# S5 coefficients of C in two buffers, the Toeplitz tile in a shared staging ring, and part of the mLSTM norm on ScalarE

## The chip, the cores and the metric

One core of one Trainium2 chip runs the whole kernel. The time is device microseconds (us) of one execution, inputs and outputs in the chip's memory; lower is better. The kernel before was timed three times. Each engine (TensorE or PE, VectorE or DVE, ScalarE or ACT, GpSimd or POOL, SyncE or SP) works through its own list of instructions in order; DMAs are issued from the lists of SP and ACT.

## What is computed

One step of a two-layer streaming encoder for 16 meta tokens, 2048 prompt frames and 8 sample streams of 16 frames. Layer 0 projects u = rmsnorm(x) into an S5 branch and an mLSTM branch with their gates; layer 1 has a retention and an RG-LRU branch. The parts that the change touches, cut to their core:

```python
# S5: complex diagonal state space, 32 groups of 16 channels, 64 states
_, _, h_re, h_im = lax.associative_scan(_cplx_combine, (a_re, a_im, bu_re, bu_im), axis=1)
y = einsum('btgp,gcp->btgc', h_re, c_re) - einsum('btgp,gcp->btgc', h_im, c_im)
y = gelu(y + d * u)
y = y * sigmoid(y @ w_glu + b_glu)
# mLSTM: 4 heads of 256, head norm over the head's 256 channels
mu = mean(h); var = mean(square(h - mu))
y = (h - mu) * rsqrt(var + EPS) * norm_w + skip * xc      # then times silu(zb)
```

## The kernel before, in words

The phases are the layer-0 projections of the S5 operands (`phase_in0`), the layer-0 projections of the mLSTM operands with the S5 branch woven in (`phase_l0`), the mLSTM chunks (`phase_mlstm`), the output projection (`phase_out0`) and layer 1 (`phase_in1`, `phase_ret`). Outside `phase_mlstm`, where PE's list is written out by hand, a scheduler of the framework sets the order of every engine's list from the program's dependencies and a model of durations, and the buffers of a tile name are handed out in the order in which the program asks for them.

**The projections of `phase_l0`.** The tokens are cut into six blocks (`ub`), two to a third. For each third and each of 8 column tiles `m` there are an xb part and a z part (`mtile`, L369 to L430): a weight slice is loaded by SP (L379), split by ACT and POOL into two fp32r halves, and for each block 8 × 3 matmuls of 384 columns (`mm3`, L121 to L125) fill a PSUM tile `pm`. The blocks of u come back from memory in `reload` (L461): three loads of 512 KB by SP (L467) into `ut1`, a ring of 4 buffers of 128×1024, then a cast on ACT (L105) and a subtraction on DVE (L109). `reload(2)` is called in the first third after m = 4, `reload(3)` at the beginning of the second third, after the first-block halves of two tiles.

**S5.** `s5` (L765) is a generator that is stepped once per tile from the third tile on (L506 to L510), so 14 steps belong to the first third: eight of the scan (loads, transposes L820, matmuls L827 into `ee`, scan on DVE L803 to L810), one that writes the states out (L836 to L863), and five of the eight y steps. The y part first loads C (L868, real and imaginary, each with transposes L871 and a copy L872) and d (L880, L881). For each q of 8, `toeplitz(q)` (L884) does:

- four small scalings into `cp` (L888 to L891), three DVE operations of 128×1088 into `ca` and a temporary (L895, L897, L899): the coefficients of C times powers;
- four matmuls (L904) into PSUM `pk`, a copy by ACT into `kp`, the d term on DVE (L908), and by SP one DMA of `kp` to memory (L909) and 8 DMAs back into the Toeplitz tile `tz` (L912), which shift each row.

The y loop (L916) then runs 20 matmuls per q (L925 to L931) on `tz`, `ca`, `ur` and `ee`, copies the result to `yst` and writes it out by ACT (L935). In the third third comes the GLU: loads of y (L950), the GLU weight into two buffers of the same ring `ut1` (`room`), Gelu, and projections with `mm3`.

**mLSTM.** Per chunk of 128 tokens, `ml_score_steps` builds scores, state weights and g = skip × xc on POOL (L1253). `ml_normed` (L1258) finds the head's mean and variance on DVE, rstd by a power on POOL (L1269), −mean × rstd on POOL (L1270), and y = scale × num + bias on ACT (L1271). `ml_gated_steps` adds and gates: DVE L1292 per k, then POOL multiplies by the gate for all 8 k at once (L1296).

Of the kernel before, what the change touches and what calls it, by code (L numbers as in the profile page):

```python
# [9 lines left out]
F32 = mybir.dt.float32  # L10
F32R = mybir.dt.float32r
I32 = mybir.dt.int32
AF = mybir.ActivationFunctionType
OP = mybir.AluOpType
# [9 lines left out]
KD = 8  # L24
# [329 lines left out]
def phase_l0(e):  # L354
# [103 lines left out]
    s5g = s5(e, ps)  # L458
    e.s5.loaded = False
    e.s5.room = lambda: xp.tile([128, 1024], F32R, name="ut1", bufs=4)  # L460
    def reload(bi):  # L461
        blk, b0, n = blks[bi]
        pool = e.ub_pool if bi % 3 < 2 else sb
        t = e.ub[bi] = pool.tile([128, 2, KD, 384], F32R, name=f"ub{bi % 3}", bufs=1)
        for c, nt, kind, row in blk:
            ur = xp.tile([128, KD, 128], F32, name="ut1", bufs=4)[:, :, :nt]
            nc.sync.dma_start(ur, e.u[:, :, c:c + nt])  # L467
            split(nc, t[:, 0, :, c - b0:c - b0 + nt], t[:, 1, :, c - b0:c - b0 + nt], ur)
# [296 lines left out]
def s5(e, ps):  # L765

    nc, v, tc = e.nc, e.nc.vector, e.tc
    p = e.s5
# [92 lines left out]
    with P(e, "s5y", side="right") as sb:  # L861

        pw, cc = p.pw, p.b  # L863
        for j, nm in enumerate(("re", "im")):
            cr = sb.tile([128, 4, 17, 16], F32, name="s5tm2").rearrange("p a b c -> p (a b c)")
            cr = cr[:, :512].rearrange("p (a b c) -> p a b c", a=4, b=2)
            for q in range(2):
                nc.sync.dma_start(cr[:, :, q, :], e.i["s5_c_" + nm].rearrange("a (m g) c p -> (g c) (a m) p", m=4))  # L868
            pc = ps.tile([128, 4, 128], F32, name="s5p", bufs=3)
            for m in range(4):  # L870
                nc.tensor.transpose(pc[:, m, :], cr[:, m].rearrange("p a b -> p (a b)"), e.ident)  # L871
            v.tensor_copy(cc[j].rearrange("p (m g) c -> p m (g c)", m=4), pc)  # L872


        d16 = sb.tile([128, 8], F32, name="s5d16")
        dd = sb.tile([128, 8, 16], F32, name="s5dd")
        v.memset(dd, 0.0)
        for j in range(4):
            js = slice(32 * j, 32 * j + 16)
            nc.sync.dma_start(d16[js], e.i["s5_d"].rearrange("a (q j c) -> j c (a q)", c=16, j=4)[j])  # L880
            v.tensor_tensor(dd[js], e.ident[js, None, js].to_broadcast([16, 8, 16]),  # L881
                            d16[js, :, None].to_broadcast([16, 8, 16]), op=OP.mult)

        def toeplitz(q):  # L884
            ur = s5_u(e, sb, q)
            gs = slice(4 * q, 4 * q + 4)
            cp = sb.tile([128, 2, 4, 17], F32, name="s5cp")
            v.tensor_copy(cp[UP, 0], pw[UP, 0, gs])  # L888
            v.tensor_scalar(cp[LO, 0], pw[LO, 1, gs], -1.0, None, op0=OP.mult)
            v.tensor_scalar(cp[UP, 1], pw[UP, 1, gs], -1.0, None, op0=OP.mult)  # L890
            v.tensor_scalar(cp[LO, 1], pw[LO, 0, gs], -1.0, None, op0=OP.mult)  # L891
            ca = sb.tile([128, 4, 17, 16], F32, name="s5ca")
            tmp = sb.tile([128, 4, 17, 16], F32, name="s5tm2")
            sh = [128, 4, 17, 16]
            v.tensor_tensor(ca, cp[:, 0, :, :, None].to_broadcast(sh), cc[0][:, gs, None, :].to_broadcast(sh),  # L895
                            op=OP.mult)
            v.tensor_tensor(tmp, cp[:, 1, :, :, None].to_broadcast(sh), cc[1][:, gs, None, :].to_broadcast(sh),  # L897
                            op=OP.mult)
            v.tensor_add(ca, ca, tmp)  # L899
            kp = sb.tile([128, 23, 16], F32, name="s5kp")  # L900
            v.memset(kp[:, 0:7, :], 0.0)
            pk = ps.tile([128, 256], F32, name="s5p", bufs=3)
            for j in range(4):
                nc.tensor.matmul(pk[32 * j:32 * j + 32], p.bb[:, 4 * q + j:4 * q + j + 2, :].rearrange("p a b -> p (a b)"),  # L904
                                 ca[:, j, 0:16, :].rearrange("p a b -> p (a b)"), start=True, stop=True,
                                 tile_position=(0, 32 * j), skip_group_check=True)
            nc.scalar.copy(kp[:, 7:23, :], pk.rearrange("p (a b) -> p a b", b=16))
            v.tensor_add(kp[:, 7, :], kp[:, 7, :], dd[:, q, :])  # L908
            nc.sync.dma_start(e.kp[q], kp)  # L909
            tz = sb.tile([128, 4, 16, 16], F32, name="s5tz")  # L910
            for k in range(8):
                nc.sync.dma_start(tz[16 * k:16 * (k + 1)],  # L912
                                  e.kp[q].rearrange("(g c) a b -> c g a b", g=4)[:16, :, 7 - k:23 - k, :])
            return ur, ca, tz

        for q in range(8):  # L916
            ur, ca, tz = toeplitz(q)
            for mh in range(2):
                yst = sb.tile([128, 4, NCH], F32, name="s5yst")
                for g0 in (0, 2):  # L920
                    py = ps.tile([128, 2, NCH], F32, name="s5p", bufs=3)
                    for j in range(2):
                        g = g0 + j
                        t0 = tz[:, g, 0:8, :].rearrange("p a b -> p (a b)")
                        t1 = tz[:, g, 8:16, :].rearrange("p a b -> p (a b)")  # L925
                        if mh == 0:
                            nc.tensor.matmul(py[:, j, :], t0, ur[:, 0, g, :], start=True, stop=False)
                        else:
                            nc.tensor.matmul(py[:, j, :], t1, ur[:, 0, g, :], start=True, stop=False)
                            nc.tensor.matmul(py[:, j, :], t0, ur[:, 1, g, :], start=False, stop=False)  # L930
                        nc.tensor.matmul(py[:, j, :],  # L931
                                         ca[:, g, 1 + 8 * mh:9 + 8 * mh, :].rearrange("p a b -> p (a b)"),
                                         ee[:, 4 * q + g, :], start=False, stop=True)
                    nc.scalar.copy(yst[:, g0:g0 + 2, :], py)
                nc.scalar.dma_start(e.ys[q // 2, mh, :, 4 * (q % 2):4 * (q % 2) + 4, :], yst)  # L935
            yield
    cls(e, "s5ee", "s5kb", "s5keep", "s5par")
    while not p.loaded:
# [200 lines left out]
def ml_score_steps(e, sb, lp, hp, pt, slots, res):  # L1139
# [67 lines left out]
    for i, slot in enumerate(slots):  # L1207
# [42 lines left out]
        p = c.p = sb.tile([128, H, 128], F32, name="m_p", bufs=nb(2))  # L1250
        v.tensor_tensor(p[:n, :, :n], pS[:n, :, :n], w[:n, :, :n], op=OP.mult)
        g = c.g = sb.tile([128, KD, 128], F32, name="m_kt" if dec else "m_g", bufs=nb(2))
        nc.gpsimd.tensor_tensor(g[:, :, :n], c.xc, e.pc[:, :, sk:sk + 1].to_broadcast([128, KD, n]), op=OP.mult)  # L1253
        res.append(c)
        yield

# [1 line left out]
def ml_normed(e, c, h, pn):  # L1258

    nc, v = e.nc, e.nc.vector  # L1260
    n, r0 = c.n, c.r0
    st = c.sb.tile([128, 6], F32, name="m_st", bufs=4)
    sm = c.sb.tile([128, 8], F32, name="m_sm", bufs=4)
    v.bn_stats(st[:n], pn[:n, 0:256])
    v.bn_aggr(sm[:n, 0:2], st[:n])
    v.tensor_scalar(sm[:n, 2:3], pn[:n, 256:257], -1.0, e.emcol[:n, r0 + h:r0 + h + 1], op0=OP.mult, op1=OP.max)
    v.tensor_scalar(sm[:n, 3:4], pn[:n, 256:257], sm[:n, 2:3], math.sqrt(EPS), op0=OP.max, op1=OP.mult)
    v.tensor_scalar(sm[:n, 4:5], sm[:n, 3:4], sm[:n, 3:4], sm[:n, 1:2], op0=OP.mult, op1=OP.add)
    nc.gpsimd.tensor_tensor(sm[:n, 5:6], sm[:n, 4:5], e.mhalf[:n, 0:1], op=OP.pow)  # L1269
    nc.gpsimd.tensor_scalar(sm[:n, 6:7], sm[:n, 0:1], sm[:n, 5:6], -1.0, op0=OP.mult, op1=OP.mult)  # L1270
    nc.scalar.activation(c.yn[:n, h, :], pn[:n, 0:256], AF.Identity, scale=sm[:n, 5:6], bias=sm[:n, 6:7])  # L1271


def ml_gated(e, c):
# [4 lines left out]
def ml_gated_steps(e, c):  # L1279

    nc, v = e.nc, e.nc.vector
    nw, g, n = e.row["ml_norm_w"], c.g, c.n
    zb = c.sb.tile([128, KD, 128], F32, name="m_rw" if c.dec else "m_zb", bufs=1 if c.dec else 2)
    nc.sync.dma_start(zb[:, :, :n], e.zb[:, :, c.c0:c.c0 + n])
    for q in range(2):
        py = c.pt("pa", 4, 128)
        for j in range(4):
            k = 4 * q + j
            nc.tensor.transpose(py[:, j, :n], c.yn[:n, k // 2, 128 * (k % 2):128 * (k % 2 + 1)], e.ident[:n, :n])
        for j in range(4):  # L1290
            k = 4 * q + j
            v.scalar_tensor_tensor(g[:, k, :n], py[:, j, :n], e.pc[:, k, nw:nw + 1], g[:, k, :n],  # L1292
                                   op0=OP.mult, op1=OP.add)
        if q == 0:
            yield
    nc.gpsimd.tensor_tensor(zb[:, :, :n], g[:, :, :n], zb[:, :, :n], op=OP.mult)  # L1296
    nc.scalar.dma_start(e.gb[:, :, c.c0:c.c0 + n], zb[:, :, :n])


# [872 lines left out]
```

## Time and profile before

| what | value |
|---|---|
| median of 3 runs | 3088.95 us (3086.74 to 3089.72) |
| the profiled execution: its time | 3077.24 us |
| its span, first to last instruction | 3075.5 us |
| mean granted TensorE clock, of 1 | 0.992 |
| PE busy | 2979.3 us, 97% of the span |
| DVE, ACT, POOL busy | 1671.9, 1059.5, 982.1 us |
| chain that ended last | PE 61%, DVE 6%, DMA 4%, ACT and POOL 1% each |

How to read it: the profile is one execution; it took 1.7 us more than its span and 11.7 us less than the median. PE is the engine with the least idle time, so a microsecond counts when PE stands still for it. The granted clock is a share of 2.4 GHz. In the tables of rows, "idle" is the time in which an engine stood still just before an instruction, with what released it.

### The profile page before, as it was taken

Reading aid. Unit: us, or ns where it says so; the run is one execution under the profiler, and the core shown is the slowest. Engines: PE = TensorE matmul, PEld = TensorE weight load, DVE = VectorE, ACT = ScalarE, POOL = GpSimd, SP = SyncE. Lnnn points to the kernel's source line nnn. Section 1 sums busy time; section 2 is a strip of 40 time slices with the busy share of each in tenths; the row PEclk is TensorE's granted clock in tenths of the full one; section 3 lists DMA queues with packets and bytes.
Section 4 is the critical chain, followed back from the end, with each engine's and each line's share of the span. In section 5 each row is a group of like instructions: output and inputs, shape, how many; then the busy total and the mean of one; then the engine's idle time right before and its main releaser. Section 6 shows DMA issues by size and latency. Waiting matters only on the chain.

```text
span 3075.5 us, 45329 instructions
## 1 busy us (share of the span) xinstructions
PE 2979.3 (97%) x17435; PEld 2696.1 (88%) x17435; DVE 1671.9 (54%) x3410; ACT 1059.5 (34%) x1860; POOL 982.1 (32%) x1160
## 2 busy tenths in 40 slices
PE   8999999998999989999999999999999999999999
PEld 7999989987988877777899999999998897888887
DVE  4845884454537772333446677767700036656563
ACT  4213443435254533211235555555511122121111
POOL 6305655445336751111111111111100024433431
PEclk9999999998999999999999999999999999999999
DMA  6447455556735557564441111111122167544442
GB/s 206 155 104 222 154 165 166 167 158 149 223 101 172 184 152 249 161 196 149 154 127 52 52 52 52 47 51 48 44 80 80 49 189 220 149 130 122 139 121 75
DMA packets 447298, 404.81 MB, mean 132 GB/s; under 512 B 43593, under 2 KB 392977, under 8 KB 447082
## 3 DMA queue, kind: packets, MB, share of 16 engines
q1 hardware_dynamic: 335340, 272.36, 31.2%
q10 hardware_dynamic: 111742, 129.56, 12.5%
q8 instruction: 137, 2.24, 0.3%
q14 instruction: 79, 0.65, 0.1%
HBM read 266.35 MB, written 135.49 MB: 131 GB/s over the span
## 4 chain that ended last, share of the span: by engine, by line
PE 61%; DVE 6%; DMA 4%; ACT 1%; issue 1%; POOL 1%; SPq 0%; DVEq 0%; POOLq 0%; ACTq 0%
PE p_pm L124 9%; PE p_pm L125 8%; PE p_pm L123 8%; PE r_pm L125 4%; PE r_pm L124 4%; PE r_pm L123 4%; PE pa L123 3%; PE pa L124 3%; PE pa L125 3%; PE pc L1388 1%; DVE p_d L1754 1%; PE pn L1385 1%; DVE p_xc L550 1%; PE r_o L1956 1%; DMA d_gb<-m_zb 1%
## 5 line engine op out<-in xcount | busy, mean ns | idle before, releaser
L123 PE MATMUL p_pm<-pu,p_wh 128*128 128x384 f32 (+1 forms) x1568 | 512.1, 327 | 0.2 <-ACT pu L105 0.2
L124 PE MATMUL p_pm<-pu,p_wh 128*128 128x384 f32 (+1 forms) x1568 | 511.8, 327 | 0.0
L125 PE MATMUL p_pm<-pu,p_wl 128*128 128x384 f32 (+1 forms) x1568 | 511.4, 326 | 0.0
L123 PE MATMUL pm<-ub,wh 128*128 128x384 f32 (+1 forms) x1136 | 377.2, 333 | 2.0 <-ACT vo L452 1.8
L124 PE MATMUL pm<-ub,wh 128*128 128x384 f32 (+1 forms) x1136 | 376.4, 331 | 1.6 <-DVE ub L109 1.6
L125 PE MATMUL pm<-ub,wl 128*128 128x384 f32 (+1 forms) x1136 | 372.9, 331 | 2.3 <-POOL wl L118 1.9
L123 PEld LDWEIGHTS p_pm<-pu,p_wh 128*128 128x128 f32 x1568 | 294.2, 188 | 1.8 <-issue 1.2
L124 PEld LDWEIGHTS p_pm<-pu,p_wh 128*128 128x128 f32 x1568 | 294.5, 188 | 1.0 <-issue 0.8
L125 PEld LDWEIGHTS p_pm<-pu,p_wl 128*128 128x128 f32 x1568 | 294.4, 188 | 0.0
L118 POOL TENSOR_TENSOR wl<-wr,wh 128x256 fp32r<-128x256 f32 x188 | 177.8, 976 | 203.7 <-ACT wh L105 203.7
L123 PEld LDWEIGHTS pm<-ub,wh 128*128 128x128 f32 x1136 | 214.4, 189 | 7.8 <-issue 4.0
L123 PE MATMUL r_pm<-roh,r_gh 128*128 128x512 f32 x544 | 218.8, 403 | 1.2 <-ACT roh L105 0.8
L125 PE MATMUL r_pm<-roh,r_gl 128*128 128x512 f32 x544 | 217.5, 401 | 1.5 <-DVE r_gl L109 1.5
L125 PEld LDWEIGHTS pm<-ub,wl 128*128 128x128 f32 x1136 | 214.4, 189 | 4.7 <-POOL wl L118 2.6
L124 PE MATMUL r_pm<-rol,r_gh 128*128 128x512 f32 x544 | 217.9, 401 | 0.4 <-DVE rol L109 0.4
L124 PEld LDWEIGHTS pm<-ub,wh 128*128 128x128 f32 x1136 | 214.7, 189 | 3.1 <-DVE ub L109 2.1
L109 POOL TENSOR_TENSOR p_wl<-p_wr,p_wh 128x1024 fp32r<-128x1024 f32 x34 | 81.8, 2406 | 385.2 <-ACT p_wh L105 385.2
L109 POOL TENSOR_TENSOR p_xcl<-p_xc,p_xch 128x384 fp32r<-128x384 f32 (+1 forms) x48 | 46.8, 976 | 245.5 <-ACT p_xch L105 209.0
L125 PEld LDWEIGHTS r_pm<-roh,r_gl 128*128 128x128 f32 x544 | 103.3, 190 | 24.0 <-DVE r_gl L109 2.4
L123 PEld LDWEIGHTS r_pm<-roh,r_gh 128*128 128x128 f32 x544 | 103.1, 190 | 22.7 <-ACT roh L105 1.3
L124 PEld LDWEIGHTS r_pm<-rol,r_gh 128*128 128x128 f32 x544 | 103.2, 190 | 21.0 <-DVE rol L109 0.7
L1754 DVE RECIPROCAL p_d<-p_d 128x384 f32<-128x384 f32 (+1 forms) x48 | 116.7, 2432 | 0.6
(731 smaller groups left out, 6751.0 us busy)
## 6 DMA issues: line engine op xcount, KB each, us to landing
wr<-in_ev_w_in_dram SPq DMA_DIRECT2D x47, 512.0 KB
p_wr<-in_od_w_in_dram SPq DMA_DIRECT2D x40, 512.0 KB
d_in<-p_o ACTq DMA_DIRECT2D x80, 192.0 KB
m_rw<-d_grow SPq DMA_DIRECT2D x18, 512.0 KB
s5u<-d_ua SPq DMA_DIRECT2D x32, 274.0 KB
d_v<-vo ACTq DMA_DIRECT2D x68, 128.0 KB
m_va<-d_v SPq DMA_DIRECT2D x17, 512.0 KB
d_h<-o_x ACTq DMA_DIRECT2D x17, 512.0 KB
```

The costliest lines, as they stand in the source:

```text
L109: (nc.gpsimd if pool else nc.vector).tensor_tensor(l, x, h, op=OP.subtract)
L118: nc.gpsimd.tensor_tensor(out[:, c], a[:, c], b[:, c], op=op)
L123: nc.tensor.matmul(out, a[0], b[0], start=start, stop=False, **kw)
L124: nc.tensor.matmul(out, a[0], b[1], start=False, stop=False, **kw)
L125: nc.tensor.matmul(out, a[1], b[0], start=False, stop=stop, **kw)
L550: v.tensor_scalar(out, x(3), pc[:, m, cw + 3:cw + 4], pc[:, m, cb:cb + 1], op0=OP.mult, op1=OP.add)
L1385: nc.tensor.matmul(pn[:n], c.qs[:, 2 * h + k, :n], ct[h][:, k, :], start=False, stop=k == 1)
L1388: nc.tensor.matmul(pc, c.kw[:n, h, 128 * k:128 * (k + 1)], c.va[:n, h, :], start=True, stop=True)
L1754: v.reciprocal(d[:, :n], d[:, :n])
L1956: nc.tensor.matmul(po, qk[:, h, :], S[:, h, :], start=False, stop=True)
```

## The change

Five edits in the S5 and mLSTM code:

1. `ca` gets two buffers instead of one.
2. `tz` no longer has a buffer of its own (`s5tz`, one buffer) but is taken from `e.s5.stage`, which hands out a buffer of the `ut1` ring, the ring of the reloads.
3. `yst` holds two groups instead of four, in two buffers; y is written out by 4 DMAs per q instead of 2 (32 instead of 16).
4. In the mLSTM, POOL's g product and POOL's gate product are each done in two halves; the first half of the gate product is issued before the step's yield.
5. −mean × rstd moves from POOL to ACT as two operations: −mean (needs only the mean), then times rstd.

```diff
@@ phase_l0
     e.s5.room = lambda: xp.tile([128, 1024], F32R, name="ut1", bufs=4)
+    e.s5.stage = lambda: xp.tile([128, 1024], F32, name="ut1", bufs=4)
@@ s5, toeplitz(q)
-            ca = sb.tile([128, 4, 17, 16], F32, name="s5ca")
+            ca = sb.tile([128, 4, 17, 16], F32, name="s5ca", bufs=2)
...
-            tz = sb.tile([128, 4, 16, 16], F32, name="s5tz")
+            tz = p.stage().rearrange("p (g a b) -> p g a b", g=4, a=16)
@@ s5, y loop
             for mh in range(2):
-                yst = sb.tile([128, 4, NCH], F32, name="s5yst")
                 for g0 in (0, 2):
+                    yst = sb.tile([128, 2, NCH], F32, name="s5yst", bufs=2)
...
-                    nc.scalar.copy(yst[:, g0:g0 + 2, :], py)
-                nc.scalar.dma_start(e.ys[q // 2, mh, :, 4 * (q % 2):4 * (q % 2) + 4, :], yst)
+                    nc.scalar.copy(yst, py)
+                    gs = slice(4 * (q % 2) + g0, 4 * (q % 2) + g0 + 2)
+                    nc.scalar.dma_start(e.ys[q // 2, mh, :, gs, :], yst)
@@ ml_score_steps
-        nc.gpsimd.tensor_tensor(g[:, :, :n], c.xc, e.pc[:, :, sk:sk + 1].to_broadcast([128, KD, n]), op=OP.mult)
+        for q in range(2):
+            qs = slice(4 * q, 4 * q + 4)
+            nc.gpsimd.tensor_tensor(g[:, qs, :n], c.xc[:, qs], e.pc[:, qs, sk:sk + 1].to_broadcast([128, 4, n]),
+                                    op=OP.mult)
@@ ml_normed
+    nc.scalar.mul(sm[:n, 6:7], sm[:n, 0:1], -1.0)
     nc.gpsimd.tensor_tensor(sm[:n, 5:6], sm[:n, 4:5], e.mhalf[:n, 0:1], op=OP.pow)
-    nc.gpsimd.tensor_scalar(sm[:n, 6:7], sm[:n, 0:1], sm[:n, 5:6], -1.0, op0=OP.mult, op1=OP.mult)
-    nc.scalar.activation(c.yn[:n, h, :], pn[:n, 0:256], AF.Identity, scale=sm[:n, 5:6], bias=sm[:n, 6:7])
+    nc.scalar.activation(sm[:n, 7:8], sm[:n, 6:7], AF.Copy, scale=sm[:n, 5:6])
+    nc.scalar.activation(c.yn[:n, h, :], pn[:n, 0:256], AF.Identity, scale=sm[:n, 5:6], bias=sm[:n, 7:8])
@@ ml_gated_steps, per q
+        qs = slice(4 * q, 4 * q + 4)
+        nc.gpsimd.tensor_tensor(zb[:, qs, :n], g[:, qs, :n], zb[:, qs, :n], op=OP.mult)
         if q == 0:
             yield
-    nc.gpsimd.tensor_tensor(zb[:, :, :n], g[:, :, :n], zb[:, :, :n], op=OP.mult)
```

The ring's buffers go round in the order of the calls, so five `tz` now stand between the three loads of `reload(2)` and those of `reload(3)`. The lists show what the scheduler makes of it; line numbers of the S5 part are higher by one in the changed kernel. **SP's list** around the second third's reload; `ut_3875`, `ut_3879`, `ut_3883` are `reload(2)`, `ut_4945`, `ut_4949`, `ut_4953` are `reload(3)` before:

```order
L467 DMA ut_3875<-d_u 128x8x128
L467 DMA ut_3879<-d_u 128x8x128
L467 DMA ut_3883<-d_u 128x8x128
L467 DMA ut_4945<-d_u 128x8x128
L761 DMA s5u<-d_ua 128x548 x2
L779 DMA s5rt<-d_rot 128x2x516
L379 DMA wr_2863<-in_ev_w_in_dram 128x8x128
L379 DMA wr_3056<-in_ev_w_in_dram 128x8x128
L467 DMA ut_4949<-d_u 128x8x128
L441 DMA wv_3500<-in_ml_wv_dram 128x2x256
L467 DMA ut_4953<-d_u 128x8x128
```

After the change `reload(3)` is `ut_4965`, `ut_4969`, `ut_4973`, and `ut_4628` and `ut_4837` are the `tz` of q = 3 and q = 4:

```order
L913 DMA ut_4628<-d_kp 16x4x256 x8
L762 DMA s5u<-d_ua 128x548 x2
L910 DMA d_kp<-s5kp 128x368
L913 DMA ut_4837<-d_kp 16x4x256 x8
L468 DMA ut_4965<-d_u 128x8x128
L468 DMA ut_4969<-d_u 128x8x128
L468 DMA ut_4973<-d_u 128x8x128
L762 DMA s5u<-d_ua 128x548 x2
```

The loads of block 3 moved from right behind those of block 2, in the midst of the S5 scan, to behind the round trips of q = 0 to 4. **PE's list** where the y of a q ends and where `pk` of another stands, before:

```order
L929 MATMUL s5p<-s5u,s5tz 128x137
L930 MATMUL s5p<-s5u,s5tz 128x137
L931 MATMUL s5p<-s5ee,s5ca 128x137
L124 MATMUL pm_5675<-ub_3874,wh_5667 128x384
...
L125 MATMUL pm_5701<-ub_4944,wl_5668 128x384
L427 MATMUL pg_4871<-xc_5656,gw 8x192
L904 MATMUL s5p<-s5ca,s5bb 32x256 x4
L427 MATMUL pg_4871<-xc_5656,gw 8x192 x3
```

After the change, from the last projection on block 2 (`ub_3874`) to the first on block 3 (`ub_4964`); the left-out rows hold the y of q = 0 and of q = 1 to 4, with the `pk` of q = 2 to 4 between them, and nothing else:

```order
L125 MATMUL pm_4938<-ub_3874,wl_4931 128x384
L828 MATMUL s5p<-s5u,s5bat 128x137 x8
L846 MATMUL s5p<-ident,s5bat 128x128 x2
L856 MATMUL s5p<-ident,s5fin 32x128
L872 MATMUL s5p<-ident,s5tm_4151 128x128 x4
L872 MATMUL s5p<-ident,s5tm_4160 128x128 x4
L905 MATMUL s5p<-s5ca,s5bb 32x256 x4
L928 MATMUL s5p<-s5u,ut_4203 128x137
...
L905 MATMUL s5p<-s5ca,s5bb 32x256 x4
L928 MATMUL s5p<-s5u,ut_4348 128x137
...
L905 MATMUL s5p<-s5ca,s5bb 32x256 x4
L123 MATMUL pm_4977<-ub_4964,wh_4894 128x384
```

The pieces of S5 that lay between projections moved into one run of rows with no projection between them. **DVE's list** after the change, around the coefficients of the next q (`s5cp`, `s5ca`) and the d term (`s5dd`) of the q before it:

```order
L902 MEMSET s5kp 128x112
L896 TENSOR_TENSOR s5ca<-s5cp,s5b_1471 128x1088
L900 TENSOR_TENSOR s5ca<-s5ca,s5tm_4614 128x1088
L889 COPY s5cp<-s5pw 64x68
L890 TENSOR_SCALAR s5cp<-s5pw 64x68
L891 TENSOR_SCALAR s5cp<-s5pw 64x68
L909 TENSOR_TENSOR s5kp<-s5kp,s5dd 128x16
L892 TENSOR_SCALAR s5cp<-s5pw 64x68
```

Two products and three scalings for a later q now stand ahead of the d term, L909, that releases the round trip.

## Rows read from the trace of the kernel before

**Rows 1.** The page, part 1: busy us (share of the span) and instructions.

```profile
PE 2979.3 (97%) x17435; PEld 2696.1 (88%) x17435; DVE 1671.9 (54%) x3410; ACT 1059.5 (34%) x1860; POOL 982.1 (32%) x1160
```

**Rows 2.** Waits of PE, whole span: line waited for, us in total, times, longest.

```profile
PE pm L123 <- ACT xb L397: 11.8, 3, 5.6
...
PE pn L1383 <- ACT m_yn L1271: 8.7, 3, 4.8
...
PE s5p L845 <- DVE s5bat L842: 4.0, 1, 4.0
...
PE pa L1248 <- DVE m_g L1292: 2.6, 4, 0.9
```

**Rows 3.** Timeline of PE, 425 to 434 us: start, duration, instruction, [idle before].

```profile
425.40 0.33 PE L123 MATMUL pm<-ub,wh 128*128 128x384 f32 x1
...
431.69 2.03 PE L827 MATMUL s5p<-s5u,s5bat 128*128 128x137 f32 x16
```

**Rows 4.** Timeline of DVE, 415 to 502 us.

```profile
415.36 1.22 DVE L109 TENSOR_TENSOR ub<-ut,ub 128x1024 fp32r<-128x1024 f32 x1
...
436.32 1.02 DVE L803 TENSOR_TENSOR s5tm<-s5ee,s5rt 64x516 f32<-64x516 f32 x1
...
451.34 1.03 DVE L842 TENSOR_TENSOR s5bat<-s5tm,s5ed 128x256 f32<-128x256 f32 x1
...
474.73 1.29 DVE L897 TENSOR_TENSOR s5tm<-s5cp,s5b 128x1088 f32<-128x1088 f32 x1
...
477.57 1.28 DVE L899 TENSOR_TENSOR s5ca<-s5ca,s5tm 128x1088 f32<-128x1088 f32 x1
```

**Rows 5.** Timeline of SP's queue, 465 to 644 us.

```profile
465.58 0.97 SPq L868 DMA_DIRECT2D s5tm<-in_s_c_im_dram  x2
...
487.91 5.08 SPq L912 DMA_DIRECT2D s5tz<-d_kp  x8
...
508.69 0.32 SPq L909 DMA_DIRECT2D d_kp<-s5kp  x1
...
511.71 5.49 SPq L912 DMA_DIRECT2D s5tz<-d_kp  x8
...
638.36 0.32 SPq L909 DMA_DIRECT2D d_kp<-s5kp  x1
640.21 3.60 SPq L912 DMA_DIRECT2D s5tz<-d_kp  x8
```

**Rows 6.** Waits of SP's queue, 400 to 700 us.

```profile
SPq L868 <- PE s5p L871: 4.0, 1, 4.0
```

**Rows 7.** Timeline of PE, 495 to 499 us: the y of q = 0.

```profile
495.17 0.47 PE L927 MATMUL s5p<-s5u,s5tz 128*128 128x137 f32 x2 [1.21 <-DMA s5tz<-d_kp]
...
498.42 0.42 PE L123 MATMUL pm<-ub,wh 128*128 128x384 f32 x1
```

**Rows 8.** PE by line, 425 to 600 us: busy us, mean ns | idle before.

```profile
L904 PE MATMUL s5p<-s5ca,s5bb 128*32 128x256 f32 x40 | 3.7, 389 | 0.0
```

**Rows 9.** Stretches: window, us, busy us PE, PEld, DVE, ACT, POOL, PEclk, DMA share, GB/s.

```profile
693.00:770.00 77.00, 62.67 (x425) 58.03 (x424) 33.98 (x55) 45.65 (x82) 44.60 (x80) 0.89 0.67 146
705.00:727.00 22.00, 9.13 (x46) 7.46 (x47) 5.71 (x13) 13.80 (x21) 8.70 (x16) 0.61 1.07 196
825.00:840.00 15.00, 15.00 (x89) 14.94 (x88) 12.73 (x37) 2.43 (x4) 5.38 (x7) 1.00 1.10 336
```

**Rows 10.** Timeline of PE behind the longest idle time of that stretch.

```profile
722.32 0.59 PE L123 MATMUL pm<-wvh,xbh 128*128 128x264 f32 x1 [5.03 <-ACT xb L397]
722.70 0.42 PE L124 MATMUL pm<-wvl,xbh 128*128 128x264 f32 x1
...
726.46 0.28 PE L123 MATMUL pm<-wvh,xbh 128*128 128x264 f32 x1
```

**Rows 11.** POOL by line, 850 to 1165 us, the mLSTM chunks: busy us, mean ns | idle before.

```profile
L1253 POOL TENSOR_TENSOR m_g<-m_xc,pc 128x1024 f32<-128x1024 f32 (+1 forms) x17 | 31.7, 1866 | 13.7 <-PE pm L125 13.7
L1270 POOL TENSOR_SCALAR m_sm<-m_sm 128x1 f32<-128x1 f32 (+1 forms) x68 | 19.6, 290 | 4.2
```

## The prediction

> **What bounds the kernel now.** Page first: PE is busy 97% of the span [rows 1], so what PE waits for is the next view. Its waits are short and few [rows 2]: of those that the change touches there are 4.0 us for the S5 state-out (L845), 8.7 us for the normed value of the mLSTM (L1383 behind ACT's L1271) and 2.6 us for the gated one (L1248). No line of the change stands in a long wait, so there is little to win. What can be lost is larger: PE's list is fixed, and in `phase_l0` the S5 branch is cheap only because projections lie between its pieces. The timelines of PE, DVE and SP from 425 us on show that: after `kp` is sent off, `tz` is there only some 9 us later [rows 5], and PE spends those with projections. Look in the rows at the times between one engine's last piece and the next engine's first.
>
> **Part 1, the reload behind the round trips.** The ring has four buffers, handed out in the program's order: three to `reload(2)`, then five to `tz` of q = 0 to 4, then three to `reload(3)`. Its loads so stand in SP's list behind the fifth round trip, and the first projection on block 3 stands in PE's list behind y(q = 4). Between the last projection on block 2 and that one, PE's list has only S5, each piece waiting for the one before. All times are from the span's start.
>
> - *Where it begins.* Before, PE goes to the third tile of the second third at 425.4 [rows 3]. After, it stands there before the last scan. Its matmuls (L827) take 2.03 [rows 3]; they begin after ACT's copies, at about 429 (estimate: the place of q = 7 in the lists), and the two copies of `ee` follow by 431.5. The last scan and the state-out on DVE last from 436.32 to 452.37, 16.05, of which 1.5 was a convolution [rows 4]: 14.5, so T = 446 (443 to 448).
> - *T to y(q = 0).* The load of imaginary C was issued at 465.58, 13.2 behind the end of L842 (452.37), of which 4.0 was a wait for PE [rows 5, 6]: T + 9.2. Landing 2.2 (the last of the first `tz` DMAs was issued by 492.99 and y began at 495.17 [rows 5, 7]), transposes and copy 1.3, the products L897 and L899 1.29 and 1.28 [rows 4]: T + 15.3. In DVE's list the scalings and two products of q = 1 stand ahead of the d term L908 of q = 0: 3.4 plus 0.2, and 0.6 for what ACT and PE put between: T + 19.5. Then the round trip D: from `kp`'s issue to the first of 8 `tz` issues 1.85 to 3.02, the issues 3.60 to 5.49, landing 2.2 [rows 5]. Of the eight pairs three lie near 1.9 and five at 2.6 to 3.0, and where SP has nothing else the issues take 3.6, so I take 2.7 + 3.6 + 2.2: D = 8.5 (7.65 to 10.7). y(q = 0) begins at T + 28 = 474 (26 to 33 behind T).
> - *Each further link.* Between 495.17 and 498.42, 14 of y's 20 matmuls run, 0.232 each, so the whole takes 4.64 at full clock [rows 7]. After an idle time the clock was low: in 705 to 727 the granted clock is 0.61, and after 5.03 of idle the same matmul shows 0.42 instead of 0.28 until 726.3, four us later [rows 9, 10]. A y that begins after a wait I put at 6.6: 4 us at half speed, then 2.64 (4.64 to 9.3). Behind it on DVE, since `ca` has two buffers and the new coefficients need that of q − 2: two products of 1.29 [rows 4] ahead of the d term, then 0.8 for `pk`'s rest, the copy and L908, then D. 6.6 + 2.6 + 0.8 + 8.5 = 18.5 (15.7 to 23.4). Four of them: 74, so y(q = 4) begins at 548.
> - *The reload.* Its three loads go out right behind the last `tz`, 2.2 ahead of y(q = 4). 1.57 MB take 4.7 us at the 336 GB/s of one stretch and 10.8 at the 146 of another [rows 9]; the queue is otherwise empty, so I take 7, nearer the first. Cast 1.05 (estimate, near the subtraction's) and subtraction 1.22 [rows 4]. PE goes on at 548 − 2.2 + 7 + 2.3 = 555.1 (553 to 559).
> - *What of it isn't lost.* PE did S5 work there that it needn't do later: L827 2.03, six `pk` at 0.74 (3.7 for five in that stretch [rows 8]) 4.4, five y at 4.64 23.2, small transposes some 2: 31.6.
>
> Net: 555.1 − 425.4 − 31.6 = **+98.1**.
>
> On the longest piece the Trainium skill, "DMA: Bandwidth & Descriptors", section "Anatomy of one DMA — SWDGE (gpsimd) path", gives one DMA about 2.0 us fixed, mostly the receipt, plus bytes over 436 GB/s. The landing of 2.2 agrees with it; by it D would be 2.0 + 3.6 + 2.0 = 7.6, five links 4.5 less, and the median below some 4.5 lower.
>
> **Part 2, what goes away.** The wait for the state-out, 4.0 [rows 2], and the 1.21 before the first y [rows 7] lie inside the new stall: −5.2.
>
> **Part 3, later S5.** The y of q = 5 to 7 still go by the ring, but with projections between them: +3 (0 to 8), the 8 being one D. `yst` in two halves costs 16 more issues on ACT; ACT is busy 34% and those lie beside PE: 0. If that cover goes, each is some 0.4 (the issue time of SP's DMAs, 3.60 / 8 [rows 5]), so 16 × 0.4 = 6 on ACT, in the stall's slack. Cold clock at the restart: 4 us at half speed, +2 (0 to 4) [rows 10].
>
> **Part 4, mLSTM.** POOL loses 68 instructions of 0.29 us [rows 11] in a chain power, product, ACT; ACT gets two small ones, of which one waits for nothing that PE needs. The halves of L1253 (1.87 each time [rows 11]) let the power in between them, and the first half of the gate product overlaps DVE's second. All of this can win at most what PE waits there, 8.7 + 2.6 = 11.3 [rows 2]; I take half, −6 (0 to −11.3). Could it lose? The extra ACT operation with the scale waits for the power and stands ahead of the next evictions: 68 of an estimated 0.2 to 0.3, in a chain that loses 0.29 in exchange; nothing net.
>
> **The sum.** 98.1 − 5.2 + 3 + 2 − 6 = +92 on 3077.24: 3169. The profiled execution lies 11.7 below the median; the same difference on the median gives 3088.95 + 92 = **3181**.
>
> **The rivals.**
>
> 1. *Shorter links (3144).* D at its lower end and less, as SP has nothing else in its list there: 8 issues at 0.3 each 2.4, both landings 1.85: 6.1, and each y at 4.64; so a link is 2.4 + 2.0 = 4.4 less; four links and the first D: −20. And the GLU, whose loads come earlier, no longer leaves PE idle in 693 to 770, where 77.00 − 62.67 = 14.3 are [rows 9]. 92 − 20 − 14 − 3 = 55. For: the stretch is empty of other transfers. Against: `kp`'s landing took 2.7 in most of the eight, some in quiet stretches.
> 2. *Longer links (3212).* The clock stays low for all five y and the small transposes (9.3 instead of 6.6 or less, five times, +13), D at 10 (+7), the GLU's loads now stop PE too (32 issues at 0.35, up to +11). 92 + 31 = 123: 3212. For: 0.61 of clock in a stretch with idle times of 5 us [rows 9]. Against: y is 4 us long, and there is other work at either end.
> 3. *Faster (3058).* The S5 branch is ready earlier, so the GLU is under the projections and PE loses none of the 14.3 [rows 9], nor 5.2 of S5 waits, nor 11.3 in the mLSTM: −31. It decides only if the chain up to the block-3 loads ends before PE runs out of its own work: T to restart must cost no more than 31 of real work plus 31 saved, by about 488. T is 446, so five links would need to fit in 42 us with the first already 28: 3.5 us a link, below the bare landing and y. Near impossible by rows 5.
> 4. *No change (3083).* The moved loads don't stop PE, as if blocks 2 and 3 were still loaded together. Only the −6 is left. PE's list speaks against it: nothing but S5 stands there.
>
> **How the numbers follow.** The forecast, with its own range 3156 to 3200, gets 0.68; shorter links 0.15; longer 0.12; faster 0.03; no change 0.02. The predicted time is 3181. The range goes to the nearer rivals: 3145 to 3219 leaves out little of the shorter and the far end of the longer, with the cases of no change and faster. A measurement of this kernel can tell about 0.2%, 6 us, from no change. Faster by more: 0.03. Within: 0.02. Slower by more: 0.95.
>
> **What would show it.** Right: a gap in PE's rows from about 425 to 555 with only L828, L846, L872, L905 and L928 to L932 in it, granted clock well below 1, in which PE waits for `tz` from `kp` five times, some 8 to 12 us each; the loads of block 3 at about 545; PE's idle time up by some 90 to 100 us and nearly all of it there. In the mLSTM the waits of PE for L1271 under 8.7. Wrong: projections between the y pieces; the first load on block 3 near its old place; links under 13 us or over 22; an idle time of this size elsewhere, above all in the GLU or the mLSTM.

## The result, and the profile after

The changed kernel takes 3155.97 us (median of 4 runs, 3151.03 to 3160.21) against 3088.12 for the kernel before: a ratio of 1.0222 (95% interval 1.0207 to 1.0236), **67.9 us slower**. 3181 was forecast, with 3145 to 3219 as the range. The profiled execution took 3154.68 us, its span 3153.0, which is 77.5 longer than the span of before; this one lies only 1.3 below its median, where that of before lay 11.7 below the 3088.95 of the first three runs.

Page, part 1, of the changed kernel, and below it PE's waits over the whole span:

```profile
PE 2992.8 (95%) x17435; PEld 2706.2 (86%) x17435; DVE 1657.1 (53%) x3410; ACT 1090.5 (35%) x2006; POOL 959.2 (30%) x1124
```

```profile
PE s5p L928 <- DMA ut<-d_kp: 50.3, 5, 10.3
PE s5p L846 <- DVE s5bat L843: 10.1, 1, 10.1
...
PE s5p L872 <- DMA s5tm<-in_s_c_im_dram: 6.9, 1, 6.9
...
PE s5p L905 <- DVE s5ca L900: 3.4, 1, 3.4
...
PE pn L1390 <- ACT m_yn L1277: 3.7, 2, 2.7
```

PE does the same 17435 instructions. It is busy 13.5 us longer than in [rows 1] and idle 64.0 longer (3153.0 − 2992.8 = 160.2 against 3075.5 − 2979.3 = 96.2): together the 77.5. Five waits for the Toeplitz tile make 50.3, where [rows 7] show one of 1.21; with the state-out, the load of C and the coefficients the four S5 lines make 70.7. The wait for the mLSTM's normed value fell from 8.7 [rows 2] to 3.7.

The timeline of PE in the stretch (start, duration, instruction, idle before):

```profile
422.19 1.09 PE L828 MATMUL s5p<-s5u,s5bat 128*128 128x137 f32 x8
...
435.50 0.69 PE L846 MATMUL s5p<-ident,s5bat 128*128 128x128 f32 x2 [10.13 <-DVE s5bat L843]
...
444.33 1.09 PE L872 MATMUL s5p<-ident,s5tm 128*128 128x128 f32 x4 [6.85 <-DMA s5tm<-in_s_c_im_dram]
448.85 1.08 PE L905 MATMUL s5p<-s5ca,s5bb 128*32 128x256 f32 x8 [3.43 <-DVE s5ca L900]
459.40 0.80 PE L928 MATMUL s5p<-s5u,ut 128*128 128x137 f32 x2 [9.47 <-DMA ut<-d_kp]
...
466.15 0.64 PE L905 MATMUL s5p<-s5ca,s5bb 128*32 128x256 f32 x8
476.84 0.80 PE L928 MATMUL s5p<-s5u,ut 128*128 128x137 f32 x2 [10.06 <-DMA ut<-d_kp]
...
494.24 0.80 PE L928 MATMUL s5p<-s5u,ut 128*128 128x137 f32 x2 [10.20 <-DMA ut<-d_kp]
...
511.47 0.80 PE L928 MATMUL s5p<-s5u,ut 128*128 128x137 f32 x2 [10.19 <-DMA ut<-d_kp]
...
528.78 0.80 PE L928 MATMUL s5p<-s5u,ut 128*128 128x137 f32 x2 [10.34 <-DMA ut<-d_kp]
...
535.86 0.62 PE L123 MATMUL pm<-ub,wh 128*128 128x384 f32 x2 [0.24 <-ACT ub L105]
```

Five y begin 17.44, 17.40, 17.23 and 17.31 apart, and the first projection on block 3 (L123) comes 7.1 after the fifth. In the window from the first to the last of these rows the granted clock is 0.67 and PE is busy 42.2 of 114:

```profile
422.00:536.00 114.00, 42.20 (x279) 36.77 (x278) 45.76 (x90) 14.26 (x34) 1.64 (x3) 0.67 0.37 101
```

SP's queue shows what PE waits for:

```profile
452.17 0.34 SPq L910 DMA_DIRECT2D d_kp<-s5kp  x1
454.04 3.61 SPq L913 DMA_DIRECT2D ut<-d_kp  x8
...
469.49 0.32 SPq L910 DMA_DIRECT2D d_kp<-s5kp  x1
471.38 3.60 SPq L913 DMA_DIRECT2D ut<-d_kp  x8
...
526.67 2.61 SPq L468 DMA_DIRECT2D ut<-d_u  x3
```

From the issue of `kp` (452.17, 469.49) to y (459.40, 476.84) are 7.23 and 7.35 us. The loads of block 3 go out at 526.67, right behind the fifth tile's.

### The profile page after: what moved, and what is told of

It reads as the page before. It is cut to its first block, busy times and chain, and to the rows that moved or that the text cites. A ratio compares the mean times of both kernels' runs of the same rounds, so it can differ in the third digit from the quotient of the medians.

```text
span 3153.0 us, 45528 instructions
## 1 busy us (share of the span) xinstructions
PE 2992.8 (95%) x17435; PEld 2706.2 (86%) x17435; DVE 1657.1 (53%) x3410; ACT 1090.5 (35%) x2006; POOL 959.2 (30%) x1124
## 4 chain that ended last, share of the span: by engine, by line
PE 73%; DVE 13%; DMA 7%; issue 2%; ACT 2%; POOL 1%; SPq 1%; ACTq 1%; DVEq 0%; POOLq 0%
PE p_pm L124 8%; PE p_pm L123 8%; PE p_pm L125 8%; PE pm L124 5%; PE pm L125 4%; PE pm L123 4%; PE r_pm L125 4%; PE r_pm L124 4%; PE r_pm L123 4%; PE pa L123 3%; PE pa L124 3%; PE pa L125 3%; DMA m_rw<-d_grow 1%; DVE p_d L1761 1%; DVE xc L553 1%
## 5 line engine op out<-in xcount | busy, mean ns | idle before, releaser
L123 PE MATMUL p_pm<-pu,p_wh 128*128 128x384 f32 (+1 forms) x1568 | 512.1, 327 | 0.2 <-ACT pu L105 0.2
L123 PE MATMUL pm<-ub,wh 128*128 128x384 f32 (+1 forms) x1136 | 376.8, 333 | 3.6 <-ACT vo L452 2.4
L123 PEld LDWEIGHTS p_pm<-pu,p_wh 128*128 128x128 f32 x1568 | 294.2, 188 | 1.8 <-issue 0.8
L118 POOL TENSOR_TENSOR wl<-wr,wh 128x256 fp32r<-128x256 f32 x188 | 171.0, 939 | 277.7 <-ACT wh L105 273.2
L123 PEld LDWEIGHTS pm<-ub,wh 128*128 128x128 f32 x1136 | 215.1, 190 | 6.9 <-ACT vo L452 2.6
L123 PE MATMUL r_pm<-roh,r_gh 128*128 128x512 f32 x544 | 218.1, 402 | 0.0
L123 PEld LDWEIGHTS r_pm<-roh,r_gh 128*128 128x128 f32 x544 | 102.8, 189 | 21.0 <-ACT roh L105 0.3
```

The costliest lines, as they stand in the source:

```text
L118: nc.gpsimd.tensor_tensor(out[:, c], a[:, c], b[:, c], op=op)
L123: nc.tensor.matmul(out, a[0], b[0], start=start, stop=False, **kw)
```

## The experiments

All ratios are against runs of the kernel before on the same chip; the medians of before in the three sets were 3084.5, 3082.6 and 3085.2.

**Only the staging.** The kernel before, with one edit:

```diff
-            tz = sb.tile([128, 4, 16, 16], F32, name="s5tz")
+            tz = p.stage().rearrange("p (g a b) -> p g a b", g=4, a=16)
```

> The kernel before with only the Toeplitz tile taken from the reloads' ring (one buffer of the C coefficients, y written in four groups, mLSTM as before). Theory (the ring's order puts the loads of block 3 behind five round trips): the whole loss is here and somewhat more, because with one coefficient buffer all three DVE products of 1.29 us stand in each link instead of two: links of about 19 us instead of 17.3, four of them +7, so 3155 to 3175 us, PE waiting five times for the Toeplitz tile. Rival (the loss comes from the second coefficient buffer, the 32 writes of y or the mLSTM edits): below 3120 us.

3164.74 us, ratio 1.0257 (1.0237 to 1.0278): more than the whole loss from this line alone. PE's waits in 400 to 600 us, and SP's queue:

```profile
PE s5p L928 <- DMA ut<-d_kp: 44.1, 5, 9.2
PE s5p L905 <- DVE s5ca L900: 14.6, 5, 3.4
```

```profile
470.76 0.32 SPq L910 DMA_DIRECT2D d_kp<-s5kp  x1
...
490.61 0.32 SPq L910 DMA_DIRECT2D d_kp<-s5kp  x1
```

This link is 19.85 long; the four take 19.0 to 20.5, 19.9 in the mean against 17.2 in the changed kernel. The coefficients now hold up `pk` in each of the five, not once. The second coefficient buffer thus takes some 2.6 us out of each link of the changed kernel; it isn't a cause of the loss.

**The same memory, dealt out as 3 + 1.** The changed kernel with a buffer of the ring's four set apart:

```diff
-    e.s5.stage = lambda: xp.tile([128, 1024], F32, name="ut1", bufs=4)
+    e.s5.stage = lambda: xp.tile([128, 1024], F32, name="tz1", bufs=1)
```

The ring's other users get `bufs=3`, and the first of the four GLU weight tiles takes `tz1`.

> The changed kernel with the same memory dealt out otherwise: the ring has 3 buffers, and the fourth is the Toeplitz tile's own (and one of the four GLU weight tiles, later). Everything else of the change is kept. Theory: the loads of block 3 depend on no Toeplitz tile, SP's list has them ahead of the first kp again, the stall is gone and the time is 3075 to 3095 us. Rival (two coefficient buffers, the smaller y tile, or ACT's additional work cost it): stays over 3130 us.

3070.94 us, ratio 0.9959 (0.9944 to 0.9973); a second time 0.9951 (0.9939 to 0.9963):

> The kernel with the ring dealt out as 3 + 1 and all other edits, a second time, beside its two variants on the same chip: ratio 0.996, by every theory.

PE's waits in 400 to 600 us:

```profile
PE s5p L846 <- DVE s5bat L843: 4.2, 1, 4.2
...
PE s5p L928 <- DMA tz<-d_kp: 0.7, 1, 0.7
```

Five waits of 10 us have become one of 0.7, though each Toeplitz tile makes the same trip (the first `kp` goes out at 488.84, the last of its eight `tz` issues ends at 495.32). The loads of block 3 are all issued by 423.6, ahead of it. The stall belongs to the shared ring and not to the trip, and without it the change is 0.4% faster than the kernel before.

**The same sharing, asked for in another order.** S5's y steps are held until the second third:

```diff
-            if steps > 2:
+            if steps > 2 and (third or steps < 12):
```

> The changed kernel with one condition on when S5 is stepped: its y steps are held until the second third, so that the ring is asked for block 3's buffers before the first Toeplitz tile; the ring stays shared. Theory (it is the order of asking, not the sharing): no stall at 422 to 536 us, each Toeplitz tile lies between projections, 3075 to 3110 us (S5 is done later, so some may come back at the GLU). Rival (a ring shared by reloads and Toeplitz tiles is too small in any order): over 3130 us.

3078.01 us, ratio 0.9975 (0.9963 to 0.9987). Of PE's waits for a Toeplitz tile in 400 to 600 us one is left:

```profile
PE s5p L928 <- DMA ut<-d_kp: 1.2, 1, 1.2
```

A ring of four is large enough for both users; what cost the time was that five `tz` were asked for ahead of block 3.

**Three tiles instead of five.** As in the run above, but with `steps < 15`, so that three y steps stay in the first third:

> The changed kernel with S5 stepped twice less in the first third: three Toeplitz tiles instead of five are taken from the ring before block 3's loads. Theory (each such tile adds one whole round trip to what PE sits through): two links of 17.3 us less, of which two y with their pk, 2 x 5.3 at full clock, come back elsewhere as work that now lies between projections and were no loss to begin with; net of that each link loses 17.3 - 5.3 = 12, so 3156 - 24 = 3132 us (3122 to 3140). Rival (a single wait whose length doesn't depend on the number of tiles): 3150 us or more, or no stall at all (below 3095).

3132.99 us, ratio 1.0161 (1.0146 to 1.0175). The last y before block 3, its `pk` and the first projection on block 3:

```profile
495.86 0.80 PE L928 MATMUL s5p<-s5u,ut 128*128 128x137 f32 x2 [10.09 <-DMA ut<-d_kp]
...
502.27 0.64 PE L905 MATMUL s5p<-s5ca,s5bb 128*32 128x256 f32 x8
502.84 0.61 PE L123 MATMUL pm<-ub,wh 128*128 128x384 f32 x2
```

PE goes on 33.0 earlier than in the changed kernel (535.86): two links, 35.0, less the 2.0 by which the first `kp` left later (454.20 instead of 452.17). The two y and `pk` that it still has to do bring that to 22.4, and the profiled spans differ by 22.0. Each against the kernel before of its own set, the loss fell from 67.9 to 50.4, by 17.5; that 3132.99 came so close to the expected 3132 is in part luck, since the kernel before was 5.5 us faster on this chip. So the loss grows with the number of tiles, but not all of it does: the waits for the state-out, for C and for the coefficients ahead of the first y are 20.4 in the changed kernel and 20.7 here.

**The tile's DMAs on two queues.**

```diff
-                nc.sync.dma_start(tz[16 * k:16 * (k + 1)],
+                (nc.scalar if k % 2 else nc.sync).dma_start(tz[16 * k:16 * (k + 1)],
```

> The changed kernel with the 8 DMAs of each Toeplitz tile issued alternately by SP and ACT. Theory (the exposed round trip is in good part the serial issue, 3.6 us for 8): four issues instead of eight, 1.8 us less in each of five links, 9 us less: 3147 us (3142 to 3152). Rival (landing, not issue, sets the time, or ACT's issues come late because its list has other work first): 3154 us or more.

3150.08 us lies in the range that was expected, but the kernel before took 3082.6 on this chip: the ratio, 1.0223 (1.0205 to 1.0240), is that of the change, and nothing was won. It is a miss. SP, ACT and PE around the first y, and the start of each later one:

```profile
451.54 0.34 SPq L910 DMA_DIRECT2D d_kp<-s5kp  x1
453.41 1.73 SPq L913 DMA_DIRECT2D ut<-d_kp  x4
453.42 1.79 ACTq L913 DMA_DIRECT2D ut<-d_kp  x4
...
457.76 0.80 PE L928 MATMUL s5p<-s5u,ut 128*128 128x137 f32 x2 [8.45 <-DMA ut<-d_kp]
...
464.66 0.64 PE L905 MATMUL s5p<-s5ca,s5bb 128*32 128x256 f32 x8
...
474.58 0.80 PE L928 MATMUL s5p<-s5u,ut 128*128 128x137 f32 x2 [9.28 <-DMA ut<-d_kp]
...
491.39 0.80 PE L928 MATMUL s5p<-s5u,ut 128*128 128x137 f32 x2 [9.15 <-DMA ut<-d_kp]
...
508.69 0.80 PE L928 MATMUL s5p<-s5u,ut 128*128 128x137 f32 x2 [9.50 <-DMA ut<-d_kp]
...
525.87 0.80 PE L928 MATMUL s5p<-s5u,ut 128*128 128x137 f32 x2 [9.51 <-DMA ut<-d_kp]
```

The eight issues do take 1.8 us less (1.8 against 3.6), but y begins 2.55 after the last of them instead of 1.75, so `kp` to y fell by 1.0 only, 7.23 to 6.22 (by 0.7 to 1.05 in the later trips). And y took longer: 6.9 to 7.15 in all five, where it had been 6.75 and then less each time, down to 6.20. In the second y the matmuls at 0.66 to 0.67 us a pair went on for 4.2 us instead of 3.3; why they did so after a shorter wait was not tried. So the first two links are 16.8 instead of 17.4, the other two 17.3 and 17.2, no shorter than before; the fifth y begins 2.9 earlier, and of that 1.6 is the first one's start. The Trainium skill, "DMA: Bandwidth & Descriptors", section "Rules for kernel authors", says that spreading DMAs over issuers saves issue time and nothing else, since the same DMA engines move them; the trace agrees in direction, and shows that not even all of the issue time is kept.

**One coefficient buffer in the 3 + 1 kernel.** `name="s5ca", bufs=2` becomes `name="s5ca"`.

> The kernel with the ring dealt out as 3 + 1, with the second buffer of the C coefficients taken away again. Theory A (the second buffer is what makes that kernel faster than the mLSTM edits alone make it, 3071 against 3077): 3077 us. Theory B (the second buffer is worth nothing once projections lie between the y pieces, and the rest comes from the y tile in halves or the order around it): 3071 us.

3080.33 us, ratio 0.9989 (0.9978 to 1.0001), clear of both ratios with two buffers: theory A, the second buffer brings 0.3%. The last projection of `phase_l0` (the line's last start) comes at 859.2 with two buffers and 871.8 with one (the rows of the two kernels):

```profile
L123 PE MATMUL pm<-ub,wh x1136: 284/335/687, 17.0 to 859.2; 128*128 128x384 f32 x157, 128*128 128x272 f32 x33
```

```profile
L123 PE MATMUL pm<-ub,wh x1136: 283/334/689, 16.9 to 871.8; 128*128 128x384 f32 x157, 128*128 128x272 f32 x33
```

**y in whole tiles in the 3 + 1 kernel**, that is with `yst` of four groups and 16 writes as before:

> The kernel with the ring dealt out as 3 + 1, with y written out in tiles of four groups as before (16 DMAs instead of 32). Theory (once projections lie between, the y tile decides nothing): the ratio of that kernel, 0.996, within 0.001. Rival (the 16 additional issues on ACT cost some 6 us where ACT is waited for): 0.994.

3069.85 us, ratio 0.9946 (0.9933 to 0.9960), not to be told from the 0.9951 of its neighbour. The rival's 0.994 lies in the interval too, so it is shown only that the y tile decides no more than some 0.2% here. This is the fastest of the versions run, by less than its interval.

**The mLSTM edits**, alone on the kernel before, and in parts. All of them:

> The kernel before with only the mLSTM edits (norm's mean product on ScalarE, GpSimd's two products in halves). Theory: PE's waits of 8.7 us for the normed value and 2.6 us for the gated one shrink by about half, 3077 to 3088 us, about -6. Rival (ScalarE's additional operation that waits for the power delays its evictions, or the extra instructions cost on GpSimd's side): 3092 us or more.

3077.25 us, ratio 0.9979 (0.9970 to 0.9989). Only the mean product on ScalarE:

> The kernel before with only the mean product moved to ScalarE; GpSimd's products whole as before. Theory (the shorter chain behind the power is the gain): most of the 7 us of the mLSTM edits, 3078 to 3081 us. Rival (the halves let the power in and are the gain): 3083 to 3086 us.

3081.15 us, ratio 0.9997 (0.9986 to 1.0007). Only the halves:

> The kernel before with only GpSimd's two products of the mLSTM in halves; the norm as before. Theory (after the norm alone gave 0.9997: the halves are what lets the power in earlier): ratio 0.998 or lower, all of the mLSTM edits' 0.9979. Rival (the two edits only work together, since the power is late by either cause): 0.999 to 1.000.

3083.77 us, ratio 0.9993 (0.9982 to 1.0003). The halves, without the mean product, in the 3 + 1 kernel:

> The kernel with the ring dealt out as 3 + 1, with the mean product back on GpSimd and the halves kept. If the halves are the whole gain in the mLSTM: ratio 0.996 or lower as with the norm on ScalarE. If the two edits only work together: 0.9975 to 0.998.

3070.28 us, ratio 0.9953 (0.9940 to 0.9966), as with both. Alone neither part can be told from nothing, against the theory of either run; both together give 0.2% on the kernel before, and in the 3 + 1 kernel the norm's place makes no difference. Whether the two need each other stays open: the intervals touch.

## Why the prediction was right, and where its terms were off

The mechanism was the forecast one, at the place forecast: the loads of block 3 behind five round trips, in a stretch in which PE has S5 alone. The rivals "faster" and "no change" fell with the result. Of "shorter links" the direction held and the amount didn't: `kp` to y stayed over 7 us, where it asked for 6.1, and PE's idle time in 600 to 770 us was 20.4 (18.9 before). The GLU's loads of y came earlier (the first at 598.7, before at 679.1), and the stall beside them moved from 705 to 727 us [rows 9] to 620 to 640, where PE stands idle for 13.4 of 20, so the earlier GLU gave nothing back. "Longer links" fell with D. The time itself lies at the lower edge of the forecast's own range (3156 to 3200), nearer to the 3144 of "shorter links" than to 3181. And one sign was put too high: PE's idle time rose by 64.0, not by 90 to 100, while PE was busy 13.5 longer. The 25 us between 3181 and 3155.97 are terms:

| term | forecast | measured |
|---|---|---|
| T, end of the state-out | 446 (443 to 448) | 435.5 |
| T to y(q = 0) | 28 (26 to 33) | 23.9 |
| round trip D | 8.5 (7.65 to 10.7) | 7.23 to 7.64 |
| link | 18.5 (15.7 to 23.4) | 17.2 to 17.4 |
| fifth y to the first projection on block 3 | 7.1 | 7.1 |
| that projection | 555.1 | 535.86 |
| mLSTM, first `pa` to the output projection | −6 | +2.5 |

- **T, 10.5 early, is the term that was furthest off.** 429 was set for L827 by the place of q = 7 in the lists; it ran at 422.19, and DVE began at 425.81 instead of 431.5, 5.7 early. And the scan's operations were priced as in [rows 4]. The timeline of DVE after shows the same 64×516 product at 0.69 where it had been 1.02, and the whole from there to the state-out 9.6 where 14.5 was taken, 4.9 less:

```profile
425.81 0.69 DVE L804 TENSOR_TENSOR s5tm<-s5ee,s5rt 64x516 f32<-64x516 f32 x1 [7.52 <-ACT s5ee L831]
...
434.86 0.59 DVE L843 TENSOR_TENSOR s5bat<-s5tm,s5ed 128x256 f32<-128x256 f32 x1
```

 Before, POOL was busy 12.75 of the 16 us of that work, after 0.35 of 10.5 (the fifth busy column; the first row is of before, the second of after):

```profile
436.00:452.00 16.00, 12.41 (x76) 11.51 (x74) 15.79 (x22) 5.04 (x7) 12.75 (x14) 1.00 0.37 120
```

```profile
425.00:435.50 10.50, 0.37 (x4) 0.16 (x2) 9.38 (x19) 0.45 (x2) 0.35 (x2) 0.70 0.21 50
```

 The view behind [rows 4] could have told it. The next time that the product ran in the kernel before, 8 us later, POOL stood still between two of its pieces, and the product took 0.69 there too, with PE busy all the while:

```profile
444.37 0.69 DVE L803 TENSOR_TENSOR s5tm<-s5ee,s5rt 64x516 f32<-64x516 f32 x1
```

```profile
438.86 4.56 POOL L118 TENSOR_TENSOR wl<-wr,wh 128x256 fp32r<-128x256 f32 x4
446.67 3.73 POOL L118 TENSOR_TENSOR wl<-wr,wh 128x256 fp32r<-128x256 f32 x4 [3.25 <-ACT wh L105]
```

 A duration was carried from a stretch in which two engines work into one in which one does. No run changes POOL's work alone, so both traces fit POOL as the cause, but it is not shown.
- **D** was 7.23, 7.35, 7.49, 7.48 and 7.64, just under its lower bound each time: some 1.9 to the first issue, 3.6 for the eight, 1.75 to 2.2 for the landing. The sum took the middle of rows from a stretch in which SP's queue held other loads as well; here it held nothing between `kp` and the last issue. What sets the 1.9 or the 2.7 to the first issue was not tried. The upper bound of the issues was misread: the same view has 7.20 for the eight of one tile, at 560.88, not 5.49; the sum doesn't go by it. By the Trainium skill, "DMA: Bandwidth & Descriptors", section "Anatomy of one DMA — SWDGE (gpsimd) path", with about 2.0 us fixed for one DMA, the prediction had an estimate of 7.6. The page gives that figure for DMAs that GpSimd issues; for SP's the trace shows 7.2 to 7.6 for the whole trip, so the estimate was better than the 8.5.
- **The links**: y behind a wait took 6.75, later 6.2, against 6.6, the DVE products 2.6 as taken; what was over is D. From 18.5 to 17.3 over four links that is 4.6; with T (10.5) and the first y (4.1) it makes the 19.2 by which PE went on earlier than forecast. Of the first y's 4.1, 1.3 is D; the rest lies ahead of `kp`, where the load of imaginary C went out 4.9 behind T (440.36) instead of 9.2.
- **Later S5, +3, and the restart, +2**: by the first `pa` of the mLSTM the changed kernel is 74.9 late (949.9 against 875.0). The forecast's terms up to there sum to 97.9, less 19.2 is 78.7. What was measured is 3.8 smaller, and that is not taken apart.
- **mLSTM, −6**: the stage lasts from 949.9 to 1245.7, 295.8, against 293.3 before. The wait for the normed value did shrink by 5.0, and others took its place, 6.2 behind the state (L1399), 0.9 before. The stage lasted 287.8 to 295.8 in the nine profiles of kernels with all the mLSTM edits (287.8 with these edits alone), and 292.5 and 293.3 in the two with none: it scatters by more than the term. In the medians the edits alone were worth 7.3 on the kernel before, near the 6 that was taken.
- **The offset**: 11.7 between profile and median of before was carried over; it was 1.3 after. That is 10.4 of the 25, chance of one execution, and in the forecast it should have widened the range only.

The sum on the profiles: 92 − 19.2 − 3.8 + 8.5 = 77.5, as the spans have it.

## What to carry to other kernels

A buffer ring shared by two users ties their order together: buffers come round in the order of asking, so look at who asks how often before the next request that PE needs, not at how many buffers there are. Give a tile that makes a round trip through memory its own slot, or ask for the urgent one first; here the same bytes, dealt out as 3 + 1, turned 2.2% slower into 0.4% faster. And a transfer chain is free only as long as the engine's list has other work between its pieces: the diff doesn't say that, the lists do.

## What was not expected of the hardware

- The same DVE product of 64×516 took 1.02 us beside a busy POOL and 0.69 beside an idle one, the latter in both kernels.
- Eight DMAs issued on two queues in 1.8 us instead of 3.6 on one landed 2.55 instead of 1.75 after the last issue, so that only 1.0 of the 1.8 was left.
- Each of the five y began at the lower of the clock's two levels: its first matmuls took 0.80 and 0.66 to 0.67 us a pair, its last 0.40. In the first y the granted clock was 0.50 (1.2 GHz) from 459.40 to 463.20 and 0.98 (near 2.4 GHz) from there to its end. With waits of 9.5 to 10.3 between bursts of 6 to 7 us the granted clock of the stretch was 0.67, and PE's busy time rose by 13.5 over the kernel for the same instructions.
